# Rotary embedding on one core: the last stores moved to another DMA queue, two PSUM banks per ScalarE copy

## The chip, the cores and the metric

One core of one Trainium2 chip. The metric is the device time of one execution in microseconds. The span of a profile (161.4 us for the kernel before) is about 1.9 us shorter than the timed run (163.3 us); differences are the same in both to about 0.1 us.

## The reference

```python
# x: (8, 2048, 8, 64) f32;  cos, sin: (2048, 32) f32
x1, x2 = x[..., :32], x[..., 32:]
out1 = x1 * cos - x2 * sin        # cos, sin broadcast over batch and heads
out2 = x1 * sin + x2 * cos
return np.concatenate([out1, out2], axis=-1)
```

34.1 MB are read and 33.6 MB written, and each element gets two multiplications and an addition.

## The kernel before

A batch is 128 partitions x 8192 floats, 4 MB, worked in place in one of five buffers: loaded on sync's queue, rotated, stored on scalar's queue. A batch is cut into pieces of 2048 columns (UNIT), in the first and the last batch three such and two of 1024.

```python
def store(b, lo, n):
    keep(nc.scalar.dma_start(out=ov[b, :, lo : lo + n], in_=xts[b][:, lo : lo + n]))
...
# a piece, kind "A" (most of them): GpSimd makes t2 = x_swapped * sin, then
nc.vector.tensor_mul(t1, xk, cos)           # t1 in PSUM
nc.vector.tensor_add(out=xt, in0=t1, in1=t2)
# kind "B" (first piece of batches 2, 4, 5): TensorE adds, with an identity matrix, ScalarE copies back
for j in range(n // C):                     # C = 512, one PSUM bank
    o = o_pool.tile([P, C], f32, tag="o")   # ring of two banks
    cs = slice(j * C, (j + 1) * C)
    nc.tensor.matmul(o, eye, t1[:, cs], start=True, stop=False)
    nc.tensor.matmul(o, eye, t2[:, cs], start=False, stop=True)
    keep(nc.scalar.copy(xt[:, cs], o))
# kind "C" (first piece of batches 1 and 3): VectorE makes both products, TensorE adds them
...
def shares(b):                              # what one store covers
    if b == 0:
        return [HD, 7 * HD, 2 * UNIT]
    if b == last:
        return [2 * UNIT, UNIT, UNIT]       # 2 MB, 1 MB, 1 MB
    return [ROW]                            # 4 MB
```

(Calls are shortened to what matters.)

## Time and profile before

| | before |
|---|---|
| median of three runs | 163.35 us (163.27 to 163.38) |
| span of the profile | 161.4 us |
| DMA queues' share of 16 engines | 49.8% + 48.4% |
| last DVE addition ends | 153.3 us |
| last store issued, landed | 153.3, about 160.6 us |

The rows over 40 slices and the queue table, shown in the prediction, are the ones to read first. A digit is the busy share of one fortieth of the span, about 4 us, in tenths. A queue's share is the time its packets took, over the span times 16 engines: a sum near 100% says that the sixteen engines were almost never without work. (In a short window a share can pass 100%, because a packet is counted whole where it starts.) One view more: the issues within a narrow window, which give one store's time from issue to landing. Here is the kernel before, from 152.9 to 153.6 us (source and target, issuing engine, count, size, microseconds to landing):

```profile
out_dram<-xt ACTq DMA_DIRECT2D x1, 1024.0 KB, 7.3
```

The last store needs 7.3 us though 1 MB at 433 GB/s is 2.4 us. The gap is what the change goes after.

### The profile page before, as it was taken

Reading aid. Unit: us, or ns where it says so; the run is one execution under the profiler, and the core shown is the slowest. Engines: PE = TensorE matmul, PEld = TensorE weight load, DVE = VectorE, ACT = ScalarE, POOL = GpSimd, SP = SyncE. Lnnn points to the kernel's source line nnn. Section 1 sums busy time; section 2 is a strip of 40 time slices with the busy share of each in tenths; the row PEclk is TensorE's granted clock in tenths of the full one; section 3 lists DMA queues with packets and bytes.
Section 4 is the critical chain, followed back from the end, with each engine's and each line's share of the span. In section 5 each row is a group of like instructions: output and inputs, shape, how many; then the busy total and the mean of one; then the engine's idle time right before and its main releaser. Section 6 shows DMA issues by size and latency. Waiting matters only on the chain.

```text
span 161.4 us, 467 instructions
## 1 busy us (share of the span) xinstructions
PE 46.4 (29%) x80; PEld 18.5 (11%) x80; DVE 140.1 (87%) x66; ACT 14.4 (9%) x24; POOL 139.0 (86%) x70
## 2 busy tenths in 40 slices
PE   0000000498008960893029912980000000000000
PEld 0000000133003420340014401430000000000000
DVE  0468899999999999999999999999899998999900
ACT  3200000013000220032001210140000000000000
POOL 1299999999999899998996999998999979999200
PEclk9999999999955696599755985799555555555555
DMA  5999999899999999999999999999999999999995
GB/s 181 418 445 464 449 430 390 373 427 499 406 390 447 430 487 390 447 438 414 447 422 430 447 416 438 447 406 447 455 392 455 447 398 455 438 406 455 410 398 231
DMA packets 3458, 67.65 MB, mean 419 GB/s; under 512 B 384, under 2 KB 384, under 8 KB 768
## 3 DMA queue, kind: packets, MB, share of 16 engines
q1 hardware_dynamic: 1728, 34.08, 49.8%
q10 hardware_dynamic: 1728, 33.56, 48.4%
q14 instruction: 2, 0.02, 0.0%
HBM read 34.08 MB, written 33.55 MB: 419 GB/s over the span
## 4 chain that ended last, share of the span: by engine, by line
DMA 46%; DVE 37%; POOL 9%; issue 2%; SPq 1%; DVEq 0%; POOLq 0%; ACTq 0%
DMA xt<-in_x_dram 24%; DVE t L128 18%; DMA out_dram<-xt 18%; DVE xt L135 17%; POOL t L121 9%; DMA sin_sb<-in_sin_dram 3%; DVE t L145 1%; SPq L69 0%; SPq L67 0%; DVEq L135 0%; POOLq L121 0%; ACTq L74 0%
## 5 line engine op out<-in xcount | busy, mean ns | idle before, releaser
L121 POOL TENSOR_TENSOR t<-xt,sin_sb 128x1024 f32<-128x1024 f32 (+1 forms) x32 | 70.4, 2200 | 10.7 <-DMA sin_sb<-in_sin_dram 5.7
L128 DVE TENSOR_TENSOR t<-xt,cos_ps 128x2048 f32<-128x2048 f32 (+1 forms) x34 | 73.4, 2166 | 0.8
L121 POOL TENSOR_TENSOR t<-xt,nsin 128x1024 f32<-128x1024 f32 (+1 forms) x32 | 70.4, 2200 | 0.0
L135 DVE TENSOR_TENSOR xt<-t,t 128x2048 f32<-128x2048 f32 (+1 forms) x29 | 62.2, 2144 | 6.2 <-POOL t L121 3.7
L140 PE MATMUL o<-t,eye 128*128 128x512 f32 x24 | 17.1, 803 | 25.2 <-DVE t L128 25.2
L156 PE MATMUL o<-t,eye 128*128 128x512 f32 x16 | 10.9, 781 | 36.8 <-DVE t L128 36.8
L141 PE MATMUL o<-t,eye 128*128 128x512 f32 x24 | 15.0, 710 | 0.0
L142 ACT COPY xt<-o 128x512 f32<-128x512 f32 x12 | 7.0, 586 | 46.5 <-PE o L141 46.5
L140 PEld LDWEIGHTS o<-t,eye 128*128 128x128 f32 x24 | 5.6, 247 | 33.5 <-issue 33.5
L161 ACT COPY xt<-o 128x512 f32<-128x512 f32 x8 | 4.7, 586 | 42.6 <-PE o L157 42.6
L156 PEld LDWEIGHTS o<-t,eye 128*128 128x128 f32 x16 | 3.6, 247 | 41.7 <-POOL t L121 30.6
L141 PEld LDWEIGHTS o<-t,eye 128*128 128x128 f32 x24 | 5.9, 248 | 8.5 <-issue 8.5
L92 DVE COPY cos_ps<-cos_sb 128x512 f32<-128x512 f32 x1 | 0.7, 695 | 6.2 <-DMA cos_sb<-in_cos_dram 6.2
L157 PE MATMUL o<-t,neye 128*128 128x512 f32 x8 | 4.9, 714 | 0.2 <-DVE t L145 0.2
L145 DVE TENSOR_TENSOR t<-xt,sin_ps 128x2048 f32<-128x2048 f32 x2 | 4.6, 2279 | 0.0
L157 PE MATMUL o<-t,eye 128*128 128x512 f32 x8 | 4.1, 592 | 0.0
L157 PEld LDWEIGHTS o<-t,neye 128*128 128x128 f32 x8 | 1.8, 239 | 3.6 <-issue 3.6
L157 PEld LDWEIGHTS o<-t,eye 128*128 128x128 f32 x8 | 1.5, 190 | 1.9 <-issue 1.9
L89 ACT ACT_TABLE_LOAD x1 | 1.3, 1283 | 0.7 <-PEq L204 0.7
L89 ACT ACTIVATE nsin<-sin_sb 128x512 f32<-128x512 f32 x1 | 0.6, 629 | 4.9 <-DMA sin_sb<-in_sin_dram 4.9
L90 ACT COPY sin_ps<-sin_sb 128x512 f32<-128x512 f32 x1 | 0.6, 580 | 0.0
L79 POOL MEMSET eye<- 128x128 f32 x1 | 0.2, 205 | 0.3 <-POOLq L204 0.3
(6 smaller groups left out, 1.0 us busy)
## 6 DMA issues: line engine op xcount, KB each, us to landing
xt<-in_x_dram SPq DMA_DIRECT2D x7, 4096.0 KB, 38.9
out_dram<-xt ACTq DMA_DIRECT2D x6, 4096.0 KB, 28.3
out_dram<-xt ACTq DMA_DIRECT2D x2, 2048.0 KB, 18.9
xt<-in_x_dram SPq DMA_DIRECT2D x2, 1024.0 KB, 6.0
xt<-in_x_dram SPq DMA_DIRECT2D x1, 2048.0 KB, 11.5
out_dram<-xt ACTq DMA_DIRECT2D x2, 1024.0 KB, 8.7
out_dram<-xt ACTq DMA_DIRECT2D x1, 1792.0 KB, 20.4
cos_sb<-in_cos_dram SPq DMA_DIRECT2D x1, 256.0 KB, 5.0
```

What stands on the lines that cost most here:

```text
L89: keep(nc.scalar.mul(nsin, sin_sb, -1.0))
L92: keep(nc.vector.tensor_copy(cos_ps, cos_sb))
L121: nc.gpsimd.tensor_mul(out=t2u[:, :, u, :].rearrange("p (r h) d -> p r h d", h=H), in0=xu[:, :, 1 - u, :].rearrange("p (r h) d -> p r h d" ...
L128: nc.vector.tensor_mul(out=t1.rearrange("p (r k d) -> p r k d", r=nr, d=Dh), in0=xk, in1=rep(cos_ps[:, r0 : r0 + nr, :], 2 * H),)
L135: keep(nc.vector.tensor_add(out=xt, in0=t1, in1=t2))
L140: nc.tensor.matmul(o, eye, t1[:, cs], start=True, stop=False)
L141: nc.tensor.matmul(o, eye, t2[:, cs], start=False, stop=True)
L142: keep(nc.scalar.copy(xt[:, cs], o))
L145: nc.vector.tensor_mul(out=t2.rearrange("p (r k d) -> p r k d", r=nr, d=Dh), in0=xk, in1=rep(sin_ps[:, r0 : r0 + nr, :], 2 * H),)
L156: nc.tensor.matmul(o, eye, t1u[:, gs, u, :], start=True, stop=False)
L157: nc.tensor.matmul(o, eye if u else neye, t2u[:, gs, 1 - u, :], start=False, stop=True)
L161: nc.scalar.copy(xu[:, gs, u, :], o.rearrange("p (g d) -> p g d", d=Dh))
```

## The change

Its intent: sync's queue is idle after the last load, so the last batch's stores go there and need not wait behind batch 6 on scalar's queue; and one ScalarE copy takes two PSUM banks, to halve their number.

```diff
-    o_pool = ctx.enter_context(tc.tile_pool(name="op", bufs=2, space=PSUM))
+    o_pool = ctx.enter_context(tc.tile_pool(name="op", bufs=1, space=PSUM))
...
     def store(b, lo, n):
-        keep(nc.scalar.dma_start(out=ov[b, :, lo : lo + n], in_=xts[b][:, lo : lo + n]))
+        queue = nc.sync if b == last else nc.scalar
+        keep(queue.dma_start(out=ov[b, :, lo : lo + n], in_=xts[b][:, lo : lo + n]))
...
-            for j in range(n // C):
-                o = o_pool.tile([P, C], f32, tag="o")
-                ...
-                keep(nc.scalar.copy(xt[:, cs], o))
+            for j in range(n // (2 * C)):
+                o = o_pool.tile([P, 2 * C], f32, tag="o")
+                for k in range(2):
+                    ...                       # the two matmuls of a chunk, into half k of o
+                keep(nc.scalar.copy(xt[:, 2 * j * C : 2 * (j + 1) * C], o))
```

(Kind "C" is changed in the same way; the cuts are marked with dots.)

More of the change, by code (lines that the diff above doesn't have):

```diff
@@ L136, in rotate @@
         elif kind == "B":
-            for j in range(n // C):
-                o = o_pool.tile([P, C], f32, tag="o")
-                cs = slice(j * C, (j + 1) * C)
-                nc.tensor.matmul(o, eye, t1[:, cs], start=True, stop=False)
-                nc.tensor.matmul(o, eye, t2[:, cs], start=False, stop=True)
-                keep(nc.scalar.copy(xt[:, cs], o))
+            for j in range(n // (2 * C)):
+                o = o_pool.tile([P, 2 * C], f32, tag="o")
+                for k in range(2):
+                    cs = slice((2 * j + k) * C, (2 * j + k + 1) * C)
+                    oc = o[:, k * C : (k + 1) * C]
+                    nc.tensor.matmul(oc, eye, t1[:, cs], start=True, stop=False)
+                    nc.tensor.matmul(oc, eye, t2[:, cs], start=False, stop=True)
+                keep(nc.scalar.copy(xt[:, 2 * j * C : 2 * (j + 1) * C], o))
         else:
@@ L152, in rotate @@
             for u in range(2):
+                o = o_pool.tile([P, n // 2], f32, tag="o")
                 for j in range(n // 2 // C):
-                    o = o_pool.tile([P, C], f32, tag="o")
+                    oc = o[:, j * C : (j + 1) * C]
                     gs = slice(j * G, (j + 1) * G)
-                    nc.tensor.matmul(o, eye, t1u[:, gs, u, :], start=True, stop=False)
+                    nc.tensor.matmul(oc, eye, t1u[:, gs, u, :], start=True, stop=False)
                     nc.tensor.matmul(
-                        o, eye if u else neye, t2u[:, gs, 1 - u, :], start=False, stop=True
+                        oc, eye if u else neye, t2u[:, gs, 1 - u, :], start=False, stop=True
                     )
-                    keep(
-                        nc.scalar.copy(
-                            xu[:, gs, u, :], o.rearrange("p (g d) -> p g d", d=Dh)
-                        )
+                keep(
+                    nc.scalar.copy(
+                        xu[:, :, u, :], o.rearrange("p (g d) -> p g d", d=Dh)
                     )
+                )
     def pieces(b):
```

## The prediction

> **What bounds the kernel now.** I read the 40-slice rows first, then the queue table, the chain that ended last, and the busy table by stage. The page shows three candidates at once: DVE 87% busy, POOL 86%, and the DMA engines.
>
> ```profile
> span 161.4 us, 467 instructions
> PE 46.4 (29%) x80; PEld 18.5 (11%) x80; DVE 140.1 (87%) x66; ACT 14.4 (9%) x24; POOL 139.0 (86%) x70
> ...
> DVE  0468899999999999999999999999899998999900
> ...
> DMA  5999999899999999999999999999999999999995
> ...
> q1 hardware_dynamic: 1728, 34.08, 49.8%
> q10 hardware_dynamic: 1728, 33.56, 48.4%
> ...
> HBM read 34.08 MB, written 33.55 MB: 419 GB/s over the span
> ```
>
> DVE ends two slices before the span does; the DMA row is full from the second slice to the last but one, and the two queues' packets fill 98.2% of all 16 engines' time. So it is bytes that end this kernel. The busy table by stage (window, its length, busy time of PE, PEld, DVE, ACT, POOL, clock, DMA share, GB/s) gives the rate, and with it an account of the whole span:
>
> ```profile
> 20.00:60.00 40.00, 19.21 (x32) 7.48 (x32) 39.10 (x18) 4.69 (x8) 39.42 (x18) 0.87 1.00 423
> 60.00:100.00 40.00, 18.66 (x33) 7.50 (x33) 39.14 (x19) 4.69 (x8) 37.45 (x17) 0.74 1.01 433
> ...
> 131.60:143.40 11.80, 0.00 (x0) 0.00 (x0) 11.03 (x5) 0.00 (x0) 11.69 (x6) 0.50 0.98 422
> 143.40:153.30 9.90, 0.00 (x0) 0.00 (x0) 9.49 (x6) 0.00 (x0) 6.91 (x5) 0.50 0.98 424
> 153.30:161.10 7.80, 0.00 (x0) 0.00 (x0) 0.00 (x0) 0.00 (x0) 0.00 (x0) 0.50 0.79 336
> ```
>
> Take 433 GB/s of a full middle stage as the ceiling. 67.65 MB / 433 = 156.2 us of the 161.4. The other 5.2 us: the first slice of 4.03 us ran at 181 GB/s (4.03 x (1 - 181/433) = 2.3 us lost), the last at 231 (1.9 us), and 20 to 60 us at 423 (0.9 us). Sum 5.1 us. Nothing else is lost anywhere, so a change to the tail plays for the 1.9 us of the last slice, and much of that is the last packets' ragged end, their landing and the end of the program.
>
> The tail itself: the chain in order of time names it.
>
> ```profile
> 63.05 29.56 DMA out_dram<-xt
> 92.62 0.03 SPq L67
> 92.65 0.03 issue
> 92.68 38.90 DMA xt<-in_x_dram
> ```
>
> The last load lands at 92.68 + 38.90 = 131.6 us. After that only scalar's queue moves data, and the DVE timeline has the last batch's adds end at 143.4 (after its second piece), 148.1 (third) and 153.3 (fifth), each followed at once by its store of 2, 1 and 1 MB. When the last store is issued at 153.3 every compute engine is done, yet the DMA goes on to about 160.2: that store takes 7.3 us to land, and what it waits for is bytes ahead of it in its own queue.
>
> **What the Trainium skill says.** "DMA: Bandwidth & Descriptors", section "Issuing engines are not separate DMA queues": DMAs started by scalar, sync or gpsimd run on the same 16 engines and interleave there; several issuers save only sequencer time. The trace agrees so far as it can: with both queues at work 433 GB/s, with one alone 422 and 424, no step between them beyond the few per cent by which whole packets fall in or out of a window. The same page's "Specifications" gives 435 GB/s as the fabric ceiling; 433 is there already. "ScalarE: Activation LUTs", section "What ACT_TABLE_LOAD costs": an instruction with immediate operands takes 186 ns + 0.833 ns per element, so 612 ns for 512; the trace has 586 for the PSUM copies, close. "TensorE: Matmul & The Clock Gate", section "What's actually happening": after an idle window of about 3.4 us the array is back at half clock; the trace agrees in kind, each burst of matmuls here starts slow (first copy 3.8 us after the first matmul at 49.05, later ones 1.72 us apart).
>
> **The change, part by part.**
>
> Part 1, the queue. Sync issued its last load at 92.7, so it is free, and no load stands behind the stores. Removed from scalar: three issues of 0.34 us, on an engine 9% busy: nothing. Bytes after 143.4 in the table: 9.9 x 424 + 7.8 x 336 = 4.20 + 2.62 = 6.82 MB. The last batch is 4.19 MB of it, so 2.63 MB of earlier stores are queued ahead when its first store is issued. Before: in order, 6.82 / 433 = 15.75 us. After, with an even split (my choice, both queues having packets): each gets 216 GB/s; the batch ahead ends at 143.4 + 2.63 / 0.2165 = 155.5. By then sync's queue has moved 2.63 MB too and has 1.56 MB left, which goes at full rate in 3.6 us: 159.1, just as 143.4 + 15.75 = 159.15. (The trace's 160.2 is about 1 us later for packets in flight and uneven ends; both orders pay that.) For a gain one of the engines would have to be idle before, and for a loss after. Sync's queue always holds work: its 2 MB lasts from 143.4 to about 153.1, the next MB is there from 148.2 and the last from 153.3. So part 1 is 0.0 us on the end; it only lets the batch ahead land later (17.4 us to landing becomes about 22) and the last batch's first stores earlier (12.3 becomes about 10.5).
>
> Part 2, the copies. Removed: 20 copies of 512 elements at 586 ns, 11.7 us. Added: 10 of 1024 at about 586 + 512 x 0.833 = 1013 ns (estimate from the row and the page's slope), 10.1 us. ScalarE gains 1.6 us that nobody waits for.
>
> ```profile
> L142 ACT COPY xt<-o 128x512 f32<-128x512 f32 x12 | 7.0, 586 | 46.5 <-PE o L141 46.5
> L161 ACT COPY xt<-o 128x512 f32<-128x512 f32 x8 | 4.7, 586 | 42.6 <-PE o L157 42.6
> ```
>
> Paid for it: the ring is now one buffer of two banks instead of two of one, so TensorE can't fill ahead while ScalarE drains. In batch 2's piece the copies start at 52.84, 55.72, 57.44, 59.15 and end at 59.74. After: one copy from 55.7 to 56.7, the second pair of chunks 2 x 1.72 = 3.4 us to 60.2, a second copy to 61.2: 1.5 us later, and up to 3.8 if the matmuls after the stall are at the slow 2.9 us a chunk. Who notices? The batch's store waits for its fourth piece anyway: issued at 46.8, 63.05, 81.5, 97.7 and 114.2 for batches 1 to 5, while copies would now end (same arithmetic) near 42, 61.2, 76.3, 95.6 and 110.6. All hidden; in the slow case batch 2 slips about 0.5 us, with the DMA queues full, which costs the end nothing. The other tie is the three-deep buffer of POOL's products, one of which the matmuls hold longer:
>
> ```profile
> POOL t L121 <- DMA xt<-in_x_dram: 2.8, 3, 1.1
> POOL t L121 <- DVE xt L135: 1.8, 2, 1.3
> ```
>
> POOL already gives 1.8 us in two pieces to a buffer held like that; a few tenths to 2 us more may come. But POOL also idles 0.8 and 1.1 us for the loads of batches 6 and 7, which absorbs it, and DVE's end at 153.3 has room: the last store alone would need 1.05 MB / 433 = 2.4 us plus some 2 us of issue and landing (estimate), so 157.7 at the latest need against a landing at 153.3 + 7.3 = 160.6. About 3 us of compute slip are free.
>
> Sum: 0.0 (queue) + 0.0 (copies) = 163.3 us.
>
> **The rivals.** (a) The intended one: the last store no longer stands behind batch 6 and lands in 4.4 us instead of 7.3, 2.9 us off, 160.4 us. For it: 7.3 us in the chain's last link. Against: the bytes ahead are still owed, only on the other queue; the end is when both are empty. (b) Two queues run the engines a little fuller than one: 422 to 424 rising to 433 over 29 us is 0.6 us, 162.7. For it: those table rows; against: the DMA shares of 0.98 next to 1.01 are within what whole packets do to a window. (c) Two store streams disturb each other by a per cent or two over 16 us: 0.2 to 0.3 us slower. The mixed loads and stores at 433 speak against it. (d) The single PSUM buffer holds POOL's buffers so long that DVE slips over the roughly 5 us free (3 at the end, 1.9 in waits for loads): five tiles by 3.8 us is 19 us of longer holding, though only overlap with POOL's need counts; if 7 us slipped, 165.5. The hidden ends above speak against it.
>
> **Range and chances.** 163.3 us, with (a), (b) pulling down by tenths and (c), (d) up: 162.8 to 163.9 for 8 in 10. Faster by 2% means below 160.1, more than the whole of the last slice's loss: 1%. Slower by 2% needs (d) nearly complete: 2%. Within 2%: 97%.
>
> **What would show it.** Right: DMA row full to the last slice again and about 433 GB/s; 4.19 MB moved between the queues, to about 38.3 MB on sync's and 29.4 MB on scalar's; the last store's landing still near 7 us; batch 6's store near 22 us; ten copies near 1.01 us; last DVE add within 2 us of 153.3. Wrong: DMA idle before the end while a store waits, a last DVE add after about 156.5, or a tail with both queues that moves well under 420 GB/s.

## The result, and the profile after

| | before | after |
|---|---|---|
| median | 163.33 us (6 runs) | 163.36 us (6 runs) |
| ratio of fast runs | | 0.9999, 95% interval 0.9979 to 1.0019 |
| span | 161.4 us | 161.6 us |

A ratio here is the mean time of one kernel's fast runs over that of the other's fast runs of the same rounds, so it is not quite the ratio of the medians quoted. The change is worth nothing, in either direction. These are the page's lines of the changed kernel that answer to those shown in the prediction:

```profile
span 161.6 us, 460 instructions
PE 47.2 (29%) x80; PEld 17.8 (11%) x80; DVE 140.1 (87%) x66; ACT 12.8 (8%) x14; POOL 139.0 (86%) x70
...
DVE  0468899999999999999999999999899998999900
...
DMA  5999998899999999999999999999999999999995
...
q1 hardware_dynamic: 2160, 38.27, 55.8%
q10 hardware_dynamic: 1296, 29.36, 42.2%
...
L145 ACT COPY xt<-o 128x1024 f32<-128x1024 f32 x6 | 6.1, 1012 | 45.7 <-PE o L144 45.7
L165 ACT COPY xt<-o 128x1024 f32<-128x1024 f32 x4 | 4.0, 1012 | 47.1 <-PE o L161 47.1
```

4.19 MB changed queues (33.56 to 29.36 MB on scalar's, q10), and the two shares still sum to 98.0%. The DMA row ends in the same 5. ScalarE does ten copies of 1012 ns in place of twenty of 586. The busy table by stage has the tail unchanged too (window, length, busy time of PE, PEld, DVE, ACT, POOL, clock, DMA share, GB/s):

```profile
131.60:143.40 11.80, 0.00 (x0) 0.00 (x0) 10.91 (x5) 0.00 (x0) 11.57 (x6) 0.50 0.98 425
143.40:153.30 9.90, 0.00 (x0) 0.00 (x0) 9.48 (x7) 0.00 (x0) 7.03 (x5) 0.50 0.99 425
153.30:161.10 7.80, 0.00 (x0) 0.00 (x0) 0.11 (x1) 0.00 (x0) 0.00 (x0) 0.50 0.79 334
```

Before it was 422, 424 and 336 GB/s. From 143.4 us on two queues have work where one had, and the engines move no more for it. And the last store, from 152.9 to 153.6 us of the changed kernel:

```profile
out_dram<-xt SPq DMA_DIRECT2D x1, 1024.0 KB, 7.3
```

It is on another queue (SPq for ACTq), and lands after the same 7.3 us. The two stores before it also keep their times, 12.3 and 10.0 us: each of them ends when batch 6 and the stores up to it have all moved, and that is the same sum of bytes in either kernel. Only the store of batch 6 pays, 19.4 us for 17.4. From 133.3 to 133.6 us, where it is issued, before and after:

```profile
out_dram<-xt ACTq DMA_DIRECT2D x1, 4096.0 KB, 17.4
```

```profile
out_dram<-xt ACTq DMA_DIRECT2D x1, 4096.0 KB, 19.4
```

Why the first of the moved stores gained nothing at all is in the DMA view of two windows after its issue at 143.53 us (queue, packets, MB, share of the engines):

```profile
143.53 10.24 SPq L75 DMA_DIRECT2D out_dram<-xt  x3
```

From 143.5 to 147.6 us:

```profile
q10 hardware_dynamic: 58, 1.90, 107.2%
```

From 148.4 to 150.3 us:

```profile
q10 hardware_dynamic: 16, 0.52, 63.8%
q1 hardware_dynamic: 20, 0.33, 40.2%
```

For four microseconds after the issue sync's queue (q1) does not move one packet; the packet records put its first at 147.7 us, and on half of the engines it comes at 148.5 or later (the records don't name the engine; sixteen rows of sync's start before 149, the next near 149.5). The engines go on with scalar's rows of 32 KB. Then the two queues take turns, a row of the one and a row of the other, and since sync's rows are 16 KB it gets about a third of the bytes while both have work. That lasts only about 2 us, for batch 6 has no more than one or two rows left on each engine; the last of them ends at 151.8 us.

### The profile page after: what moved, and what is told of

Same layout as the page of the kernel before. It is cut to its first block, busy times and chain, and to the rows that moved or that the text cites. A ratio compares the mean times of both kernels' runs of the same rounds, so it can differ in the third digit from the quotient of the medians.

```text
span 161.6 us, 460 instructions
## 1 busy us (share of the span) xinstructions
PE 47.2 (29%) x80; PEld 17.8 (11%) x80; DVE 140.1 (87%) x66; ACT 12.8 (8%) x14; POOL 139.0 (86%) x70
## 3 DMA queue, kind: packets, MB, share of 16 engines
q10 hardware_dynamic: 1296, 29.36, 42.2%
## 4 chain that ended last, share of the span: by engine, by line
DMA 46%; DVE 37%; POOL 9%; issue 2%; SPq 1%; DVEq 0%; POOLq 0%; ACTq 0%
DMA xt<-in_x_dram 24%; DVE t L129 18%; DMA out_dram<-xt 18%; DVE xt L136 17%; POOL t L122 9%; DMA sin_sb<-in_sin_dram 3%; DVE t L148 1%; SPq L69 0%; SPq L67 0%; DVEq L136 0%; POOLq L122 0%; ACTq L75 0%
## 5 line engine op out<-in xcount | busy, mean ns | idle before, releaser
L122 POOL TENSOR_TENSOR t<-xt,sin_sb 128x1024 f32<-128x1024 f32 (+1 forms) x32 | 70.5, 2204 | 10.8 <-DMA sin_sb<-in_sin_dram 5.8
L143 PE MATMUL o<-t,eye 128*128 128x512 f32 x24 | 16.5, 778 | 23.7 <-DVE t L129 20.2
L160 PE MATMUL o<-t,eye 128*128 128x512 f32 x16 | 10.6, 749 | 39.1 <-DVE t L129 36.9
L144 PE MATMUL o<-t,eye 128*128 128x512 f32 x24 | 14.7, 701 | 0.0
L145 ACT COPY xt<-o 128x1024 f32<-128x1024 f32 x6 | 6.1, 1012 | 45.7 <-PE o L144 45.7
L143 PEld LDWEIGHTS o<-t,eye 128*128 128x128 f32 x24 | 5.3, 244 | 32.8 <-issue 26.8
L160 PEld LDWEIGHTS o<-t,eye 128*128 128x128 f32 x16 | 3.6, 247 | 44.5 <-POOL t L122 30.6
L165 ACT COPY xt<-o 128x1024 f32<-128x1024 f32 x4 | 4.0, 1012 | 47.1 <-PE o L161 47.1
L144 PEld LDWEIGHTS o<-t,eye 128*128 128x128 f32 x24 | 5.7, 239 | 8.0 <-issue 8.0
L161 PE MATMUL o<-t,neye 128*128 128x512 f32 x8 | 6.0, 847 | 0.2 <-DVE t L148 0.2
L161 PE MATMUL o<-t,eye 128*128 128x512 f32 x8 | 4.1, 592 | 0.0
L161 PEld LDWEIGHTS o<-t,eye 128*128 128x128 f32 x8 | 1.5, 190 | 1.9 <-issue 1.9
## 6 DMA issues: line engine op xcount, KB each, us to landing
out_dram<-xt SPq DMA_DIRECT2D x1, 2048.0 KB, 12.3
```

What stands on the lines that cost most here:

```text
L122: nc.gpsimd.tensor_mul(out=t2u[:, :, u, :].rearrange("p (r h) d -> p r h d", h=H), in0=xu[:, :, 1 - u, :].rearrange("p (r h) d -> p r h d" ...
L143: nc.tensor.matmul(oc, eye, t1[:, cs], start=True, stop=False)
L144: nc.tensor.matmul(oc, eye, t2[:, cs], start=False, stop=True)
L145: keep(nc.scalar.copy(xt[:, 2 * j * C : 2 * (j + 1) * C], o))
L160: nc.tensor.matmul(oc, eye, t1u[:, gs, u, :], start=True, stop=False)
L161: nc.tensor.matmul(oc, eye if u else neye, t2u[:, gs, 1 - u, :], start=False, stop=True)
```

## The experiments

The theory: the tail is a fixed number of bytes over engines that are all busy, so neither the order of the bytes nor the queue can move the end; and the copies are hidden. The rivals: the two parts cancel; or the end is the last addition plus a fixed latency. All kernels but one (said below) gave correct results, and all figures are of fast runs unless said otherwise.

**The queue alone.** The stores' two new lines put into the kernel before, nothing else.

> Only the queue part: the last batch's stores on sync, PSUM ring as before. Theory (bytes end the kernel, each part is worth nothing): 163.3 us, within 0.3 us of before; last store still about 7.3 us to landing; first packet on sync's queue again about 4 us after its issue. Rival (the two parts cancel, the queue gains and the copies lose): clearly below before, by 0.5 to 3 us.

Measured: 163.36 us beside 163.34, ratio 0.9991 (0.9975 to 1.0008). The last store takes 7.3 us to landing, and the first packet on sync's queue comes 3.4 us after its issue on the earliest engine and near 4.9 on the median one.

**The copies alone.** The changed kernel with all stores on scalar.

```diff
-        queue = nc.sync if b == last else nc.scalar
-        keep(queue.dma_start(...))
+        keep(nc.scalar.dma_start(...))
```

> Only the PSUM part: two banks per copy, all stores on scalar. Theory: 163.3 us, within 0.3 us of before; copies end about 2 us later in batches 4 and 5, last DVE add within 0.2 us of 153.3. Rival (the parts cancel): slower than before by what the queue alone gains, 0.5 to 3 us.

Measured: 163.34 us beside the same 163.34, ratio 0.9988 (0.9972 to 1.0003). The last store takes 7.3 us here too. Both parts are nothing by themselves, so they don't cancel: gains and losses of 0.5 us or more are outside both intervals (the widest end, 0.28% of 163.3, is 0.46 us of gain for the copies alone).

**One store of 1 MB less.** The third quarter of the last batch isn't stored. The result is wrong; all computation stays.

```diff
             while outs and sum(outs[0]) <= done:
+                if b == last and outs[0][0] == 2 * UNIT:
+                    outs.pop(0)
+                    continue
                 store(b, *outs.pop(0))
```

> Wrong on purpose: the changed kernel without the store of the last batch's third quarter, 1.05 MB less written, all computation kept, last add still at about 153.4. Theory (bytes end it): 1.05 / 433 = 2.4 us less, 160.9 us, last store about 4.9 us to landing. Rival (the last add and a fixed latency behind it end the kernel): no change, 163.3.

Measured: 160.98 us beside 163.34, ratio 0.9845 (0.9826 to 0.9865): 2.4 us, the price of 1.05 MB at 433 GB/s to a tenth.

> The kernel without one store of 1.05 MB once more, because its only profile fell in the slow state. Theory: 160.9 us, last add near 153.4, last store landing about 4.9 us after its issue, DMA row full to the end.

Measured: 160.9 us beside 163.43, ratio 0.9837 (0.9819 to 0.9855); one of its four runs was slow, 165.5 us, and is left out. In its profile the last store is issued at the same moment and lands 2.5 us sooner. From the timeline, and the issues from 152.9 to 153.6 us:

```profile
153.32 0.34 SPq L75 DMA_DIRECT2D out_dram<-xt  x1
```

```profile
out_dram<-xt SPq DMA_DIRECT2D x1, 1024.0 KB, 4.8
```

So the 7.3 us of the last store were bytes ahead of it, on whichever queue, and taking bytes away is what shortens the kernel. An end set by the last addition and a fixed latency would not have moved.

**The last addition later by 2.5 us.** The last piece's multiplication is done three times, on the same data.

```diff
+        again = 2 if b == last and lo + n == ROW else 0
+        for _ in range(1 + again):
             keep(nc.vector.tensor_mul(out=t1, ...))
```

> The changed kernel with the last piece's multiplication done three times in place of once: the last add ends 2 x 1.24 = 2.5 us later, at about 155.9. Theory (bytes end it, about 3 us of compute slip are free): 163.3 to 163.5 us, last store about 4.9 us to landing. Rival (last add plus fixed latency): 2.5 us more, 165.8.

Measured: 163.38 us beside 163.34, ratio 0.9998 (0.9977 to 1.0019). The last store is issued at 155.93 in place of 153.43 and lands in 4.8 us:

```profile
155.93 0.33 SPq L75 DMA_DIRECT2D out_dram<-xt  x1
```

```profile
out_dram<-xt SPq DMA_DIRECT2D x1, 1024.0 KB, 4.8
```

2.5 us more work on the busiest compute engine, right ahead of the last store, cost nothing.

**Later by 7.7 us.** `again = 6`.

> As the run before but with six more multiplications of 1.24 us: last add at about 160.8. The slack is now used up: the last store meets an idle DMA and takes, by an estimate from the trace, about 1.0 us to its first packet, 8 packets x 0.306 us and 0.35 us to land, 3.8 us. Theory: landing near 164.7 in place of 160.7, so about 167.4 us, 4.0 more. Rival (last add plus a fixed 7.3 us): 7.4 more, 170.8.

Measured: 167.56 us beside 163.37, ratio 1.026 (1.0242 to 1.0278): 4.2 us for 7.7 (161.10 - 153.43). So 3.5 us of slip are free behind the last addition; the prediction had estimated 3. Now the DMA does idle before the end, which is how a latency-bound tail looks. The DMA row of the page and the GB/s below it (161.10 us falls into the last slice but one):

```profile
DMA  5999999999999999999998999999999999999906
GB/s 194 421 441 467 412 407 429 432 412 443 415 439 403 490 395 466 419 403 443 419 451 380 476 387 451 427 411 467 397 466 403 459 419 403 467 443 387 403 24 253
```

And the last store with nothing ahead of it:

```profile
161.10 0.33 SPq L75 DMA_DIRECT2D out_dram<-xt  x1
```

```profile
out_dram<-xt SPq DMA_DIRECT2D x1, 1024.0 KB, 3.8
```

So 3.8 us is what this store needs with nothing ahead of it; its first packet comes 0.83 us after the issue.

**The same on scalar's queue.**

```diff
-        queue = nc.sync if b == last else nc.scalar
+        queue = nc.scalar
```

> As the run with six more multiplications in the last piece, but the last batch's stores on scalar as before the change. Here the DMA idles before the last store, so its queue is empty whichever it is. Theory: the queue is worth nothing here either, 167.5 us within 0.3. Rival (a store on sync, behind no other DMA issues on its engine, starts earlier): scalar slower by some tenths of a us or more.

Measured: 167.45 us, 1.0239 of before (1.022 to 1.0258), and 3.9 us to landing. Where the DMA is idle the queue is worth nothing either: the two intervals overlap and the medians are 0.1 us apart.

**Batch 6 in rows of 8 KB.** This is about the step of the prediction that failed: it had the two queues share from the moment of the issue.

```diff
+        if b == last - 1:
+            return [UNIT] * 4
         return [ROW]
```

> Changed kernel with the batch before the last stored in four parts, rows of 8 KB in place of 32 KB. Disputed: why sync's first packet came 4.2 us after its issue and not at once. If each engine has a fixed number of packets accepted ahead (about 3.5 of 32 KB, 1.21 us each), the delay falls to about 1 + 3.5 x 0.3 = 2 us. If it is a fixed time or a fixed number of bytes, it stays near 4 us. The time in any case: 163.3 us within 0.4, because bytes and end are the same.

Measured: 163.77 us beside 163.37, ratio 1.0023 (1.0008 to 1.0038), so 0.4 us slower, and just outside the 163.3 within 0.4 that was expected. The span is 0.4 us longer than the changed kernel's. By the packet records about 0.2 us of that is the smaller rows' cost (309 ns for 8 KB is 2% more per byte than 1213 for 32 KB, over a transfer of 9.7 us at full rate). Its profile also loses 0.3 us more than the changed kernel's near 24 us, where the traces stumble (below) and this change isn't yet at work. The delay did not fall to 2 us. From 143.5 to 147.1 us, after an issue at 143.66, and then from 147.6 to 153.4:

```profile
q10 hardware_dynamic: 205, 1.54, 101.1%
```

```profile
q1 hardware_dynamic: 102, 1.67, 67.2%
q10 hardware_dynamic: 113, 0.85, 34.7%
```

The first packet of sync's queue comes 3.5 us after its issue on the earliest engine and near 4.35 on the median one, with twelve to fifteen small packets ahead of it and not three or four. (In the changed kernel the two figures are 4.2 and 4.9, with the queue alone 3.4 and 4.9: the smaller packets take some 0.6 us off the median.) So what is ahead is not a number of packets. Against the 0.83 us on idle engines it is some 3.5 us of queued work, about 95 KB an engine at 27 GB/s (an estimate: 433 / 16 = 27, times 3.5); whether bytes or time are the limit these runs don't tell. In the second window the two queues moved nearly the same number of rows (102 and 104; 9 of scalar's 113 packets are tiny completion packets) and sync twice the bytes, because its rows are now the longer ones: the turns go by packets, not by bytes.

**The first store cut otherwise.** A side question: in both traces the engines lose about 0.5 us near 24 us, early in the stores, where rows of the loads take longer than their usual 1213 ns.

```diff
-            return [HD, 7 * HD, 2 * UNIT]
+            return [2 * UNIT, 2 * UNIT]
```

> Changed kernel with the first batch stored in two halves (rows of 16 KB) in place of 256 KB, 1.75 MB and 2 MB. In both traces every engine loses about 0.4 us near 24 us, in the packet where the 2 KB rows of the first store end. If the cut of that store causes it, the stumble goes and the time falls by 0.3 to 0.4 us, to 163.0; if not, 163.3.

Measured: 163.64 us beside 163.37, ratio 1.001 (0.9996 to 1.0023), one slow run left out. A miss: the stumble does not go. By the packet records, rows of 32 KB that start between 20 and 28 us take 0.43 us an engine beyond their 1213 ns in the changed kernel (0.54 in the kernel before, 0.72 in the run with rows of 8 KB), and 1.02 us here, from 20.5 to 22.9 us. The total time doesn't tell them apart: the two profiles have moved the same 24.6 MB by 60 us. (This run's last addition also ends 2.4 us later, at 155.8 us, within the free slip.) The rows of 2 KB aren't needed for it. What causes it stays open: in both it falls on the loads' packets just ahead of the first wide store's.

**The tables on scalar's queue.**

```diff
-                keep(nc.sync.dma_start(out=cos_sb, in_=cos_src))
-                keep(nc.sync.dma_start(out=sin_sb, in_=sin_src))
+                keep(nc.scalar.dma_start(out=cos_sb, in_=cos_src))
+                keep(nc.scalar.dma_start(out=sin_sb, in_=sin_src))
```

> Changed kernel with the loads of cos and sin on scalar's queue, so that both queues feed the engines from the first microsecond. Some 2.5 us of DMA time are lost in the first 4 us, about 1.75 before the first packet and the rest in slow first packets. If the slow packets come from one queue's feeding, 0.2 to 0.5 us go; if it is a start-up cost of the engines, 163.4 as before. The theory (bytes) has no view beyond: at most 0.7 us to be had.

Measured: 163.5 us beside 163.43, ratio 0.9995 (0.9982 to 1.0008). No gain: the first 4 us move 165 GB/s for the changed kernel's 180. Two queues don't start the engines faster. No version that beats the kernel before came out of these runs.

## Why the prediction was right, and where not

- **The bound.** Right, and shown three ways: a megabyte less is 2.4 us less, 2.5 us more of DVE work is nothing, and later DVE work moves the end only when the DMA idles. The account of the 5.2 us that aren't full rate is looser than it says: it adds up because stages that it leaves out offset each other (131.6 to 153.3 us at 422 and 424 GB/s loses 0.5 us, for one, and 100 to 131.6 us at 439 wins 0.4).
- **Queue part worth 0.0.** Right as to the end: 163.36 us by itself, beside 163.34, as the Trainium skill has it ("DMA: Bandwidth & Descriptors", section "Issuing engines are not separate DMA queues"). The step by which it was worked out, an even split from 143.4 us, was wrong. It made batch 6 land in about 22 us and the first moved store in about 10.5; they took 19.4 and 12.3. In its place: 4.2 us or more until sync's queue gets its first packet, then about 2 us of turns by packets in which its shorter rows got about a third of the bytes. The end did not depend on it, because the sum of both queues is the same under any split. The wait could have been read in the kernel before: its first store, on scalar's queue behind sync's loads, is issued at 10.79 us, and from 10.8 to 14.4 us only sync's queue moves (scalar's first packet comes at 14.5):

```profile
q1 hardware_dynamic: 97, 1.59, 102.9%
```

- **Copies.** 1013 ns were estimated, 1012 measured. The copies of batch 2 ended 0.4 us later (60.17 for 59.74), where 1.5 had been worked out, and those of batches 4 and 5 2.1 us later (96.28 for 94.16, 111.24 for 109.11), inside the 1.5 to 3.8. The 0.4 is luck of the TensorE clock: in this profile a matmul takes 0.59 us in place of 1.06 from 52.4 us on, in the kernel before only from 55.1. In the run of the copies alone it is 55.1 again, and the copies end at 61.62, where 61.2 had been worked out. (The 612 ns for 512 elements are for the instruction ACTIVATE, of which the trace has one, at 630 ns; what the copies share with it is the slope, 1012 - 586 = 426 ns for 512 elements.) The waits of TensorE for the copies show what the lost double buffer costs:

```profile
PE o L143 <- ACT xt L145: 3.4, 3, 1.1
...
PE o L160 <- ACT xt L165: 2.2, 2, 1.1
...
POOL t L122 <- DVE xt L136: 1.9, 2, 1.5
```

  The figures are us in total, times, longest: 1.1 us for each of the five pieces. POOL's wait for a buffer went from 1.8 to 1.9 us, less than the few tenths to 2 us more that were allowed, and the last DVE addition began at 152.18 for 152.07 us. All stores were still issued after the fourth piece's addition, within 0.1 us of before. Hidden, as predicted.
- **Rivals.** (a) fell with the 7.3 us that stayed; (b), fuller engines by two queues, with 425 beside 424 GB/s; (c), disturbance, is not seen, 425 and 334 beside 424 and 336; (d), DVE's slip, was 0.1 us, and the free slip is 3.5 us where 3 had been estimated.

## What to carry to other kernels

When the shares of all DMA queues add up to nearly the whole span, count bytes: the long wait of the last store was work ahead of it on the engines, whichever its queue, and another queue only reordered who waits. Test it with a kernel that moves a megabyte less and one that computes some microseconds later; the two together tell a byte-bound tail from a latency-bound one, and how much slack there is. And before taking a buffer from a ring to make instructions larger, ask whether anybody waits for the engine that gets faster, and count what its producer then waits.

## What the Trainium skill lacked or had wrong

- "DMA: Bandwidth & Descriptors", section "Queues, rings and completion order", has each engine take turns between queues packet by packet, a packet being several descriptors. The runs agree on the turns, row by row (102 and 104 rows, 1.67 and 0.85 MB where rows were 16 and 8 KB); whether a row of the profile is the page's packet they don't show. It does not say how long a queue that comes second waits for its first turn behind a busy one: 3.4 to 5.3 us here, beside 0.83 us on idle engines, and in the median only 0.6 us less with packets of a quarter of the size.
- The same page's "Specifications" has about 358 GB/s as the HBM limit of one core, without a condition; the note under its table of measured bandwidth says that this is a core's share when both cores of a pair stream. The row alone misleads: this kernel, whose transfers are nearly all between HBM and SBUF, held 433 GB/s over a stage of 40 us, near the 435 GB/s of the fabric; nothing here shows what a second core at work would leave.
- No page has the stumble of 0.4 to 1 us ahead of the first wide store that most traces show between 20 and 26 us.
